# Hybrid encoder block: the branch gates' projections as seven half-size products per pair of feature tiles, in a stage of their own ahead of the mixers

## The chip, the cores and the metric

The kernel runs on one core of a Trainium2 chip. The metric is the device time of one execution in microseconds (us). The engines are named as in the profile: PE (TensorE matmuls) with PEld (its weight loads), DVE (VectorE), ACT (ScalarE), POOL (GpSimd), and SP, whose queue issues every DMA of this kernel.

## The reference

One layer of a bidirectional encoder: 1024 tokens, 1024 features, all in float32.

```
h = rms_norm(x)
q,k,v,r, lr_f,lr_b, sq,sk,sv, gate_a, gate_b = split(h @ w_in)
A = gla(q, k, v, lr_f, lr_b)            # 4 heads, both directions, chunks; rms_norm per head
A = (A * silu(r)) @ w_o_gla
B = windowed_attention(sq, sk, sv)      # 8 query heads, 2 kv heads, +-128 tokens, sinks
B = B @ w_o_swa
x = x + (sigmoid(gate_a) * A + sigmoid(gate_b) * B) @ w_out
x = x + (silu(h2 @ w1) * (h2 @ w2)) @ w_ffn_out        # h2 = rms_norm(x), 2816 wide
```

The change concerns `gate_a` and `gate_b`: 2048 of the columns of `h @ w_in`.

## The kernel before, in words

Activations lie with features on the partitions, in tiles of 128 features by 512 tokens, so that each of the 8 feature tiles has two halves s = 0, 1. Float32 products are made from fp32r parts: a tile is split into a rounded part (`wh`, `xh`: one ACT copy) and the rest (`wl`, `xl`: one DVE subtraction), and every block product is three matmuls, h·h, h·l and l·h (`mm3`, line 72). `wunit` (lines 62 to 69) loads 128 x 512 weights and splits them; the load goes into a ring of 4 buffers (`wr`), the halves into rings of 5 (`wh`, `wl`). PSUM is two pools of four banks, `mm` and `ch`.

The program runs through these stages.

1. Opening: the 16 tiles of x are loaded, scaled by the norm's gain and split. PE makes q0 and k0 behind them, then the gate codes (`lr_mm`) and the norm's statistics. 1/rms is a factor per token, `rstd`, multiplied in when a projection leaves PSUM.
2. Linear attention (GLA): 45 slots. Each slot runs some of `g_gates`, `g_scores`, `g_out`, `g_back_out` and `g_turn` for one chunk or another, a head's backward pass behind its forward one.
3. Windowed attention: 21 slots t. Step n (group g, block t) goes through `a_prep`, `a_turn`, `a_scores`, `a_probs` and `a_out` in slots n+1 to n+5; the keys are prepared in the first eight (`k_prep`, `k_turn`).
4. Merge: `prep_a(s)` loads the eight tiles of the GLA output (`lo`) and of r (`lr`), forms o·gain·r·sigmoid(r) and splits it into `oah` and `oal`; `branch_a(s)` multiplies by `w_o_gla` and by sigmoid(gate_a); `prep_b`, `branch_b` do the same for the attention; `out_proj` follows. `lo` and `lr` have two buffers each.
5. The feed-forward part. Its first layer (`ffn_in`) already computes each 2 x 2 block product (two feature tiles, two halves of tokens, two halves of the contraction) with seven half-size products on sums and differences of blocks, in place of eight.

The PE's order is the order in which the code is written (`manual_schedule`); the other engines and the SP queue get theirs from a scheduler that reads it. The attention steps leave PE little work, so `fill(n)` puts n matmuls out of a list of remaining projections (`dense`) between them. The list holds v, q1 to k3, the attention's keys, values and queries, r0 to r7 and last `ga0, gb0, ..., ga7, gb7`, 2400 matmuls in all, of which the gates are 768: 16 feature tiles of 48. What is left of the list after the last attention slot is run through by `fill(1 << 30)`, between the last `a_out` and `branch_a(0)`; in this kernel that is 191 matmuls.

Of the kernel before, what the change touches and what calls it, by code (L numbers as in the profile page):

```python
# [8 lines left out]
F32 = mybir.dt.float32  # L9
FR = mybir.dt.float32r  # L10
# [13 lines left out]
NB = 7  # L24
PAD = 672
# [4 lines left out]
def body(tc, i, out):  # L30
    nc = tc.nc
    with ExitStack() as root:
# [15 lines left out]
        def chtile(shape, dt=F32):  # L48
            return psc.tile(list(shape), dt, tag="ch", name=nm("ch"))

# [40 lines left out]
        def rsqrt(dst, v, scale, epsv, eps_t, pool, shape, tag):  # L91
            l = pool.tile(list(shape), F32, tag=tag + "l", name=nm("rl"))
            nc.scalar.activation(l, v, AF.Ln, bias=eps_t[:, 0:1], scale=scale)
            nc.scalar.activation(l, l, AF.Exp, scale=-0.5)
            t = pool.tile(list(shape), F32, tag=tag + "t", name=nm("rt"))
# [8 lines left out]
        stg = stgs.enter_context(tc.tile_pool(name="stg", bufs=4))  # L104
        pad = root.enter_context(tc.tile_pool(name="pad", bufs=1, side="right"))
        pad.tile([P, PAD // 4], F32, tag="pad", name="pad")
# [6 lines left out]
        gc = glas.enter_context(tc.tile_pool(name="gc", bufs=1))  # L113
        ini = ExitStack()
        ip = ini.enter_context(tc.tile_pool(name="ip", bufs=1))
        acc = ip.tile([P, T], F32, tag="acc", name="acc")
        def norm_stats(acc, pool):
            for s in range(2):
                v = chtile((P, HT))
                mm(v, ones, acc[:, s * HT:(s + 1) * HT], True, True)  # L120
                rsqrt(rstd[:, s * HT:(s + 1) * HT], v, 1.0 / T, EPS, epst, pool, (P, HT), "rs")

        def fgroup(units, xa, xb, nk):

            b = [mmtile(), mmtile()]
            k = 0
            for src, ku in units:
                h, l = wunit(src, ku * P)
                for kk in range(ku):
                    c = slice(kk * P, (kk + 1) * P)  # L130
                    st, sp = k == 0, k == nk - 1
                    mm(b[0], h[:, c], xa[k][0], st, False)
                    mm(b[0], h[:, c], xb[k][0], False, False)
                    mm(b[1], h[:, c], xa[k][1], st, False)
                    mm(b[1], h[:, c], xb[k][1], False, False)
                    mm(b[0], l[:, c], xa[k][0], False, sp)
                    mm(b[1], l[:, c], xa[k][1], False, sp)
                    k += 1
            return b

# [100 lines left out]
        lrS = gc.tile([98, T], FR, tag="lrS", name="lrS")  # L241
        upS = gc.tile([98, 2, 512], FR, tag="upS", name="upS")

        mask = gc.tile([P, 4, P], F32, tag="mask", name="mask")
        nc.vector.memset(mask, 1.0)
        nc.vector.memset(mask[:, :, 0:1], 0.0)
# [8 lines left out]
        def lr_out(b):  # L255
            lrf = ip.tile([96, T], F32, tag="lrf", name="lrf")
            for s in range(2):
                c = slice(s * HT, (s + 1) * HT)
                nc.vector.tensor_tensor(lrf[:, c], b[s][:96], rstd[:96, c], op=ALU.mult)
            nc.scalar.activation(lrS[0:96], lrf, AF.Copy)  # L260
            nc.vector.tensor_tensor(lrS[32:64], lrf[32:64], lrS[32:64].bitcast(F32), op=ALU.subtract)

        def x_tile(k, s):
            xr = ip.tile([P, HT], F32, tag="xr", name=nm("xr"), bufs=8)
            nc.sync.dma_start(out=xr, in_=i["xT"][k, s])
            nc.scalar.activation(xh[k][s], xr, AF.Copy, scale=g1[:, k:k + 1])  # L266
            nc.vector.scalar_tensor_tensor(xl[k][s], xr, g1[:, k:k + 1], xh[k][s].bitcast(F32),  # L267
                                           op0=ALU.mult, op1=ALU.subtract)
            a = acc[:, s * HT:(s + 1) * HT]
            sq = a if k == 0 else ip.tile([P, HT], F32, tag="sq", name=nm("sq"), bufs=3)  # L270
            nc.scalar.activation(sq, xr, AF.Square)
            if k:
                nc.vector.tensor_tensor(a, a, sq, op=ALU.add)

        with tc.manual_schedule(engines={mybir.EngineType.PE}):
            bq = [[mmtile(), mmtile()] for _ in range(2)]
            for k in range(KT):
                if k % 4 == 0:
                    us = [wunit(i["w_f"][m, k // 4]) for m in range(2)]
                c = slice((k % 4) * P, (k % 4 + 1) * P)  # L280
                for s in range(2):
                    x_tile(k, s)
# [3 lines left out]
            tri = load_const(gc, "tri", i["c_tri"], (P, P), U32)  # L286
# [3 lines left out]
            lr_mm(bl, 0)  # L290
            norm_stats(acc, ip)
            vt = chtile((P, KT, 2))
            for t in range(KT):
                mm(vt[:, t], acc[:, t * P:(t + 1) * P], ones[:, 0:2], True, True)
            lr_mm(bl, 1)
            proj_f_out("q0", bq[0])
            proj_f_out("k0", bq[1])
            rsqrt(rstdt, vt[:, :, 0], 1.0 / T, EPS, epst, ip, (P, KT), "rt")
            upr = ip.tile([98, 2, 512], F32, tag="upr", name="upr")
            nc.sync.dma_start(out=upr, in_=i["up"])  # L300
            nc.scalar.activation(upS, upr, AF.Copy)
            nc.vector.tensor_tensor(upS[64:98], upr[64:98], upS[64:98].bitcast(F32), op=ALU.subtract)
            nc.scalar.activation(upS[96:97], upr[96:97], AF.Copy)
            nc.vector.memset(lrS[96:98].bitcast(F32), 1.0)
            lr_out(bl)
# [11 lines left out]

        class Chunk:
            pass
# [3 lines left out]
        def g_gates(hd, c):  # L323
# [11 lines left out]
            nc.sync.dma_start(out=qk[:, 1], in_=scr[f"k{hd}", s][:, co:co + 256])  # L335
            z = chtile((P, 2, 256))
# [146 lines left out]
        for m in range(8):  # L483
            dense += [proj_f(f"ga{m}", 16 + m), proj_f(f"gb{m}", 24 + m)]
# [20 lines left out]
        swas = ExitStack()  # L505
        sc_ = swas.enter_context(tc.tile_pool(name="swc", bufs=1))
# [87 lines left out]
        def a_turn(g, n):  # L594
# [10 lines left out]
            a.p = sw.tile([P, 4, 384], F32, tag="p", name=nm("p"))  # L605
            a.mx = sw.tile([P, 4], F32, tag="mx", name=nm("mx"))

        def a_scores(g, n, h):
            a = att[g, n]
            w, p, mx = a.w, a.p, a.mx  # L610
# [158 lines left out]
        def gate(nme, s):  # L769
            g = btile(nme[:2])  # L770
            nc.sync.dma_start(out=g, in_=scr[nme, s])
            nc.scalar.activation(g, g, AF.Sigmoid)
# [63 lines left out]
        def wsplit(src, n):  # L836
            h = wp.tile([P, n], FR, tag="wh", name=nm("wh"), bufs=5)
            l = wp.tile([P, n], FR, tag="wl", name=nm("wl"), bufs=5)
            nc.scalar.activation(h, src, AF.Copy)  # L839
            nc.vector.tensor_tensor(l, src, h.bitcast(F32), op=ALU.subtract)  # L840
            return h, l

# [17 lines left out]

        def product(o, w, x, nk, start, stop):
            h, l = w
            for kk in range(nk):
                c = slice(kk * P, (kk + 1) * P)
                nc.tensor.matmul(o, h[:, c], x[kk][0], start=start and kk == 0, stop=False, skip_group_check=True)  # L865
                nc.tensor.matmul(o, h[:, c], x[kk][1], start=False, stop=False, skip_group_check=True)  # L866
                nc.tensor.matmul(o, l[:, c], x[kk][0], start=False, stop=kk == nk - 1, skip_group_check=True)  # L867
# [327 lines left out]
```

## Time and profile before

| | |
|---|---|
| median of 3 runs | 1697.69 us (1697.48 to 1699.71) |
| profiled execution: device time, and its span in the profile | 1697.71 us, 1695.6 us |
| busy share PE, PEld, DVE, ACT | 99%, 82%, 70%, 51% |
| matmuls | 7880 |
| opening, up to the GLA's first matmul | 0 to 53.9 us |
| the two attentions | 53.9 to 753.3 us |
| remaining projections | 753.3 to 796.6 us |
| merge and feed-forward | 796.6 to 1695.6 us |

The stages' borders are start times of PE instructions in the timeline. PE matmuls are pipelined: one of 512 columns shows some 0.39 us, but the next starts 0.227 us after it. So a busy share of PE says only that it rarely stood still for long; whether it waited is read from the distance of the starts.

### The profile page before, as it was taken

What the parts mean: (1) busy time and instruction counts of PE and PEld (TensorE: products, weight loads), DVE (VectorE), ACT (ScalarE), POOL (GpSimd) and SP (SyncE); (2) the same over time, 40 slices, a digit from 0 to 9 for tenths busy, and PEclk for the clock granted to TensorE, in tenths of its full rate; (3) what the DMA queues carried; (4) which work ended last, traced back from release to release, by engine and by line L of the source; (5) the groups of instructions that cost most, each with busy time, mean ns of one, the idle gap of its engine ahead of it and who ended that gap; (6) DMA issues with size and microseconds to landing.
All of it is one profiled execution on the core that took longest, in us unless ns stands there. A gap on an engine that the chain in (4) does not pass through costs nothing.

```text
span 1695.6 us, 23682 instructions
## 1 busy us (share of the span) xinstructions
PE 1675.2 (99%) x7880; PEld 1388.9 (82%) x7880; DVE 1179.8 (70%) x2454; ACT 867.8 (51%) x1939; POOL 0.2 (0%) x4
## 2 busy tenths in 40 slices
PE   8999999999999999999999999999999999999999
PEld 6788888888788878878888888888888888788887
DVE  7767777764577656537574468978778887779655
ACT  6554767775557565545453456633333333354443
POOL 0000000000000000000000000000000000000000
PEclk9999999999999999999999999999999999999999
DMA  6533444443543232237765645344223543496433
GB/s 196 156 112 111 121 130 135 132 143 119 177 128 108 82 106 81 82 108 249 237 200 168 192 137 180 116 128 149 88 94 131 172 157 129 138 342 200 142 106 118
DMA packets 153738, 245.85 MB, mean 145 GB/s; under 512 B 17582, under 2 KB 43054, under 8 KB 153616
## 3 DMA queue, kind: packets, MB, share of 16 engines
q1 hardware_dynamic: 153616, 244.34, 45.4%
q8 instruction: 62, 1.02, 0.3%
q14 instruction: 60, 0.49, 0.1%
HBM read 177.17 MB, written 67.11 MB: 144 GB/s over the span
## 4 chain that ended last, share of the span: by engine, by line
PE 92%; DVE 3%; ACT 3%; DMA 1%; issue 1%; SPq 0%; ACTq 0%; DVEq 0%
PE mm L72 46%; PE ch L72 8%; PE mm L1012 6%; PE mm L865 6%; PE mm L866 6%; PE mm L867 6%; PE ch L1012 5%; PE ch L866 2%; PE ch L867 2%; PE ch L865 2%; PE ch L647 1%; ACT p L636 1%; ACT p L630 1%; PE ch L474 0%; PE ch L389 0%
## 5 line engine op out<-in xcount | busy, mean ns | idle before, releaser
L66 ACT ACTIVATE wh<-wr 128x512 fp32r<-128x512 f32 (+1 forms) x256 | 159.2, 626 | 173.6 <-PE mm L72 149.2
L68 DVE TENSOR_TENSOR wl<-wr,wh 128x512 fp32r<-128x512 f32 (+1 forms) x256 | 174.6, 685 | 92.6 <-ACT wh L66 88.0
L72 PE MATMUL mm<-xh,wh 128*128 128x512 f32 x512 | 204.1, 399 | 6.5 <-ACT xh L266 6.5
L72 PE MATMUL mm<-xl,wh 128*128 128x512 f32 x512 | 204.0, 398 | 0.0
L72 PE MATMUL mm<-xh,wl 128*128 128x512 f32 x512 | 169.7, 398 | 0.0
L72 PE MATMUL mm<-wh,xh 128*128 128x512 f32 x320 | 126.7, 396 | 1.9 <-DVE st L146 1.2
L72 PE MATMUL mm<-wl,xh 128*128 128x512 f32 x320 | 127.3, 398 | 0.0
L72 PE MATMUL mm<-wh,xl 128*128 128x512 f32 x320 | 126.3, 395 | 0.0
L72 PEld LDWEIGHTS mm<-xh,wh 128*128 128x128 f32 x512 | 97.0, 190 | 23.3 <-ACT xh L266 6.5
L839 ACT ACTIVATE wh<-ws 128x512 fp32r<-128x512 f32 x88 | 55.5, 632 | 115.9 <-PE mm L866 68.0
L72 PEld LDWEIGHTS mm<-xl,wh 128*128 128x128 f32 x512 | 97.2, 190 | 17.5 <-DVE xl L267 0.5
L72 PEld LDWEIGHTS mm<-xh,wl 128*128 128x128 f32 x512 | 95.3, 190 | 16.7
L839 ACT ACTIVATE wh<-a 128x512 fp32r<-128x512 f32 x66 | 41.7, 632 | 89.8 <-PE ch L1012 42.3
L839 ACT ACTIVATE wh<-wr 128x512 fp32r<-128x512 f32 x52 | 32.9, 632 | 91.6 <-issue 49.7
L840 DVE TENSOR_TENSOR wl<-a,wh 128x512 fp32r<-128x512 f32 x66 | 45.5, 690 | 41.6 <-ACT wh L839 41.4
L72 PEld LDWEIGHTS mm<-wh,xh 128*128 128x128 f32 x320 | 60.2, 188 | 13.9 <-DVE st L146 1.6
L630 ACT ACTIVATE p<-p,nm,rs 128x384 f32<-128x384 f32 (+1 forms) x64 | 42.9, 672 | 56.1 <-DVE nm L624 56.1
L1012 PE MATMUL mm<-hh,wh 128*128 128x512 f32 x176 | 68.6, 390 | 1.5 <-ACT hh L984 1.5
L1012 PE MATMUL mm<-hl,wh 128*128 128x512 f32 x176 | 68.7, 390 | 0.8 <-DVE hl L985 0.8
L840 DVE TENSOR_TENSOR wl<-ws,wh 128x512 fp32r<-128x512 f32 x88 | 60.1, 683 | 12.5 <-ACT wh L839 12.5
L72 PEld LDWEIGHTS mm<-wh,xl 128*128 128x128 f32 x320 | 60.2, 188 | 10.4
L1012 PE MATMUL mm<-hh,wl 128*128 128x512 f32 x176 | 68.6, 390 | 0.1
(508 smaller groups left out, 4420.6 us busy)
## 6 DMA issues: line engine op xcount, KB each, us to landing
wr<-in_w_fi_dram SPq DMA_DIRECT2D x102, 256.0 KB, 2.8
wr<-in_w_t_dram SPq DMA_DIRECT2D x80, 256.0 KB, 2.7
wr<-in_w_f_dram SPq DMA_DIRECT2D x64, 256.0 KB, 2.7
B<-c SPq DMA_DIRECT2D x44, 256.0 KB, 2.1
T<-tx SPq DMA_DIRECT2D x44, 256.0 KB, 2.3
a<-in_w_fo_dram SPq DMA_DIRECT2D x44, 256.0 KB, 5.3
hr<-T SPq DMA_DIRECT2D x44, 256.0 KB, 2.7
hr<-B SPq DMA_DIRECT2D x33, 256.0 KB, 4.6
```

Of the source, the lines that this page charges most:

```text
L66: nc.scalar.activation(h, raw, AF.Copy)
L68: nc.vector.tensor_tensor(l, raw, h.bitcast(F32), op=ALU.subtract)
L72: nc.tensor.matmul(o, a, b, start=start, stop=stop)
L630: nc.scalar.activation(p[:, h, :w], p[:, h, :w], AF.Exp, bias=nm_[:, h:h + 1], scale=a.rs[:, h:h + 1], accum_out=dn[:, h:h + 1])
L636: nc.scalar.activation(p[:, h, :w], p[:, h, :w], AF.Copy, scale=rd[:, h:h + 1])
L647: nc.tensor.transpose(pt[:, h], a.p[:, h, (kb - a.b0) * P:(kb - a.b0 + 1) * P], ident)
L839: nc.scalar.activation(h, src, AF.Copy)
L840: nc.vector.tensor_tensor(l, src, h.bitcast(F32), op=ALU.subtract)
L865: nc.tensor.matmul(o, h[:, c], x[kk][0], start=start and kk == 0, stop=False, skip_group_check=True)
L866: nc.tensor.matmul(o, h[:, c], x[kk][1], start=False, stop=False, skip_group_check=True)
L867: nc.tensor.matmul(o, l[:, c], x[kk][0], start=False, stop=kk == nk - 1, skip_group_check=True)
L1012: nc.tensor.matmul(ys[m], a[:, c], b, start=f0, stop=f1, skip_group_check=True)
```

## The change

The sixteen gate tiles leave the list. Their products are made in a stage of their own behind the opening, for each pair (`ga` tile f, `gb` tile f) by seven products on blocks of x and w, as `ffn_in` does: `x_first(f)` makes the two that need no sums, `x_two`, `x_four` and `x_last` the five others. Sums of x are made once by `xcombos`, those of w for each pair by `w0comb`. The results go to DRAM without `rstd`, and `gate()` multiplies it in when it loads them. q0, k0 and the gate codes also go out raw (`keep_raw`), to be scaled when they are loaded. The opening loads x into 16 buffers of its own and begins with 12 small matmuls on ones; the constants and the gate-code tiles of the GLA (`lrS`, `upS`) are now allocated after the new stage, in the memory that it frees. The slots of both attentions get fewer matmuls of filling, and the windowed attention runs its steps within a slot in another order.

```diff
+        def x_first(f):
+            F = pairs[f]
+            Y = mmtile()
+            product(Y, wunit(i["w_f"][16 + f, 0]), X0["11"], 4, True, False)
+            F.p1 = ep.tile([P, HT], F32, tag=f"e{f}", name=nm("xp1")) if f < 4 else \
+                x0.tile([P, HT], F32, tag=f"xr{f - 4}1", name=nm("xp1"))
+            nc.scalar.copy(F.p1, Y)
+            product(Y, wunit(i["w_f"][16 + f, 1]), X0["21"], 4, False, True)
+            keep_raw(f"ga{f}", 0, Y)
...
+        def x_two(f):
+            F = pairs[f]
+            F.r11, F.r12, F.r21, F.r22 = (w0load(f, q) for q in (11, 12, 21, 22))
+            F.Z, F.X = chtile((P, HT)), mmtile()
+            s1 = w0comb(F.r21, F.r22, ALU.add)
+            product(F.Z, wsplit(s1, 512), X0["T1"], 4, True, False)
+            F.p5 = xtile("p5", f)
+            nc.scalar.copy(F.p5, F.Z)
+            nc.vector.tensor_tensor(F.p5, F.p5, F.p1, op=ALU.add)
+            F.s2 = w0comb(s1, F.r11, ALU.subtract)
+            product(F.X, wsplit(F.s2, 512), X0["T2"], 4, True, False)
+            F.u2 = xtile("u2", f)
+            nc.vector.tensor_tensor(F.u2, F.X, F.p1, op=ALU.add)
+
+        def x_four(f):
+            F = pairs[f]
+            s3 = w0comb(F.r11, F.r21, ALU.subtract)
+            product(F.X, wsplit(s3, 512), X0["T3"], 4, False, False)
...
+            product(F.Z, wsplit(s4, 512), X0["22"], 4, False, True)
+            nc.vector.tensor_tensor(F.u2, F.Z, F.u2, op=ALU.add)
+            keep(f"ga{f}", 1, F.u2)
+
+        def x_last(f):
+            F = pairs[f]
+            product(F.X, wsplit(F.r22, 512), X0["T4"], 4, False, True)
...
+            wu = chtile((P, 512))
+            for _ in range(12):
+                mm(wu[:, :P], ones, ones, True, True)
...
+            for f in range(NG):
+                x_first(f)
+                if f == 0:
...
+                for k in range(f, 4, 4):
+                    xcombos(k, 0)
+                for k in range(f - 4, 4, 4):
+                    if f >= 4:
+                        xcombos(k, 1)
+            for f in range(NG):
+                x_two(f)
...
+                if f:
+                    x_last(f - 1)
+                x_four(f)
+            x_last(NG - 1)
+        g0s.close()
+
+        gc = glas.enter_context(tc.tile_pool(name="gc", bufs=1))
+        lrS = gc.tile([98, T], FR, tag="lrS", name="lrS")
...
+        nc.sync.dma_start(out=upr, in_=i["up"])
+        nc.scalar.activation(upS, upr, AF.Copy)
+        nc.vector.tensor_tensor(upS[64:98], upr[64:98], upS[64:98].bitcast(F32), op=ALU.subtract)
+        nc.scalar.activation(upS[96:97], upr[96:97], AF.Copy)
...
+            nc.sync.dma_start(out=lrf[:, c], in_=scr["lr", s][:96])
+            nc.vector.tensor_tensor(lrf[:, c], lrf[:, c], rstd[:96, c], op=ALU.mult)
+        nc.scalar.activation(lrS[0:96], lrf, AF.Copy)
+        nc.vector.tensor_tensor(lrS[32:64], lrf[32:64], lrS[32:64].bitcast(F32), op=ALU.subtract)
...
-        for m in range(8):
+        for m in range(NG, 8):
             dense += [proj_f(f"ga{m}", 16 + m), proj_f(f"gb{m}", 24 + m)]
...
             fill(24)
             for t in range(last + 1):
-                n = 40 if t < 6 else 31 if t < NH * NC + 3 else 18
+                n = 40 if t < 6 else 26 if t < NH * NC + 3 else 12
...
-        order = (a_out, a_probs, a_scores, a_turn, k_turn, k_prep, a_prep)
+        order = (k_prep, a_prep, a_scores, a_turn, k_turn, a_out, a_probs)
...
-                slot([lambda e=e: e[0](*e[1:]) for e in v], 60 if t < 2 else 46 if t < 2 * KT + 2 else 28)
+                slot([lambda e=e: e[0](*e[1:]) for e in v], 36 if t < 2 else 24 if t < 2 * KT + 2 else 8)
...
+            if int(nme[2:]) < NG:
+                nc.vector.tensor_tensor(g, g, rstd[:, s * HT:(s + 1) * HT], op=ALU.mult)
             nc.scalar.activation(g, g, AF.Sigmoid)
```

Three places in the order of the engines. The first is ACT behind the gate codes. Before, it splits the first weights of the list there (`wh`), with the statistics between:

```order
L66 ACTIVATE wh_531<-wr_529 128x512
L66 ACTIVATE wh_537<-wr_535 128x512
L303 ACTIVATE upS<-upr 1x1024
L66 ACTIVATE wh_543<-wr_541 128x512
L66 ACTIVATE wh_561<-wr_559 128x512
L93 ACTIVATE rl_410<-ch_408,eps 128x512
```

Now the eight `x_first` stand there; three of them (`xp` is the copy of the first product out of PSUM, `c` that of the finished sum):

```order
L70 ACTIVATE wh_750<-wr_748 128x512
L320 COPY xp_101_638<-mm_619 128x512
L259 ACTIVATE T4h_935<-xr_302 128x512
L70 ACTIVATE wh_783<-wr_781 128x512
L309 COPY c_658<-mm_619 128x512
L70 ACTIVATE wh_803<-wr_801 128x512
L320 COPY xp_114_692<-mm_673 128x512
L70 ACTIVATE wh_836<-wr_834 128x512
L309 COPY c_712<-mm_673 128x512
L70 ACTIVATE wh_856<-wr_854 128x512
L320 COPY xp_127_746<-mm_727 128x512
```

Each copy `xp` stands behind a weight split; the ring of five gives that split (`wh_750`) the buffer that the same first product read last.

The second place is ACT in one slot of the windowed attention (`p`<-`p` with `dn`: exponentials of the four heads; `p`<-`p,rd`: division; `ph`: split of the turned probabilities; `sqh`: split of the turned queries; `sob`: the output). Before:

```order
L630 ACTIVATE p_8166,dn_8324<-p_8166,nm_8317,rs_8001 128x384
L627 ACTIVATE es_8321<-es_8321 128x4
L630 ACTIVATE p_8166,dn_8324<-p_8166,nm_8317,rs_8001 128x384 x3
L601 ACTIVATE sqh_8345<-ch_8340 128x512
L66 ACTIVATE wh_8597<-wr_8595 128x512
L636 ACTIVATE p_8166<-p_8166,rd_8330 128x384 x4
L661 COPY sob_8393<-ch_8383 128x512
L650 ACTIVATE ph_8424<-ch_8419 128x512
L650 ACTIVATE ph_8438<-ch_8433 128x512
L650 ACTIVATE ph_8451<-ch_8446 128x512
```

Now:

```order
L754 ACTIVATE sqh_8256<-ch_8251 128x512
L784 ACTIVATE p_8200,dn_8236<-p_8200,nm_8229,rs_7876 128x384
L781 ACTIVATE es_8233<-es_8233 128x4
L784 ACTIVATE p_8200,dn_8236<-p_8200,nm_8229,rs_7876 128x384 x3
L815 COPY sob_8272<-ch_8262 128x512
L790 ACTIVATE p_8200<-p_8200,rd_8242 128x384 x4
L804 ACTIVATE ph_8285<-ch_8280 128x512
L804 ACTIVATE ph_8303<-ch_8298 128x512
L804 ACTIVATE ph_8314<-ch_8309 128x512
L70 ACTIVATE wh_8593<-wr_8591 128x512
```

The three `ph` behind the division were those of the block just divided; now they are those of the block before it, which PE turned without waiting for this division.

The third place is the SP queue behind the last attention output, where the loads of `prep_a` have begun (`lo`, `lr`, `lo` stand ahead of these rows in both). Before:

```order
L755 DMA lr_9448<-r_0_5842 128x512
L771 DMA ga_9530<-ga_0_7055 128x512
L64 DMA wr_9552<-in_w_oa_dram 128x512
L771 DMA ga_9571<-ga_0_7461 128x512
L771 DMA gb_10002<-gb_0_7271 128x512
L771 DMA gb_10048<-gb_0_7646 128x512
L150 DMA ga_0_9186<-st_9187 128x512
L150 DMA ga_1_9190<-st_9191 128x512
L755 DMA lr_9460<-r_0_5943 128x512
```

Now:

```order
L909 DMA lr_9746<-r_0_8136 128x512
L925 DMA ga_9828<-ga_0_515 128x512
L925 DMA ga_9870<-ga_0_606 128x512
L68 DMA wr_9977<-in_w_oa_dram 128x512
L925 DMA gb_10308<-gb_0_1102 128x512
L925 DMA gb_10355<-gb_0_1216 128x512
L956 DMA lx_11068<-in_xT_dram 128x512
L126 DMA r_0_9682<-st_9683 128x512
L126 DMA r_1_9686<-st_9687 128x512
L909 DMA lr_9758<-r_0_8436 128x512
```

The last projection to be stored was a gate (`ga_0`, `ga_1`), with others behind it; now it is r7 (`r_0`, `r_1`), the last of the list, which the same `prep_a` needs. On PE, 50 matmuls stand between the last `a_out` and `branch_a(0)`, where 191 stood.

More of the change, by code (lines that the diff above doesn't have):

```diff
@@ L24 @@
 NB = 7
+NG = 8
 PAD = 672
@@ L263, in x_tile @@
[L263 to L271, printed above, removed]
-            if k:
-                nc.vector.tensor_tensor(a, a, sq, op=ALU.add)
+        g0s = ExitStack()
@@ new lines, in x_split, with x_square @@
+        def x_split(h, l, r, g):
+            nc.scalar.activation(h, r, AF.Copy, scale=g)
+            nc.vector.scalar_tensor_tensor(l, r, g, h.bitcast(F32), op0=ALU.mult, op1=ALU.subtract)
+        acc = [ep.tile([P, HT], F32, tag=f"e{2 + s}", name=f"acc{s}") for s in range(2)]
+        def x_square(k, s):
+            sq = acc[s] if k == 0 else ep.tile([P, HT], F32, tag=f"e{k % 2}", name=nm("sq"))
+            nc.scalar.activation(sq, xr[k, s], AF.Square)
+            if k:
+                nc.vector.tensor_tensor(acc[s], acc[s], sq, op=ALU.add)
@@ new lines, in product, with keep @@
+        def product(o, w, x, nk, start, stop):
+            h, l = w
+            for kk in range(nk):
+                c = slice(kk * P, (kk + 1) * P)
+                nc.tensor.matmul(o, h[:, c], x[kk][0], start=start and kk == 0, stop=False, skip_group_check=True)
+                nc.tensor.matmul(o, h[:, c], x[kk][1], start=False, stop=False, skip_group_check=True)
+                nc.tensor.matmul(o, l[:, c], x[kk][0], start=False, stop=kk == nk - 1, skip_group_check=True)
+        def keep(name, s, t):
+            d = scratch(f"{name}_{s}")
+            nc.sync.dma_start(out=d[:t.shape[0]], in_=t)
+            scr[name, s] = d
@@ new lines, in keep_raw @@
+        def keep_raw(name, s, b, n=P):
+            c = ep.tile([P, HT], F32, tag="c", name=nm("c"), bufs=2)
+            nc.scalar.copy(c[:n], b[:n])
+            keep(name, s, c[:n])
+        pairs = [Chunk() for _ in range(NG)]
+        def x_first(f):
[7 more added lines that the diff above has]
+            keep_raw(f"ga{f}", 0, Y)
@@ L275, in body @@
+        def x_last(f):
+            F = pairs[f]
+            product(F.X, wsplit(F.r22, 512), X0["T4"], 4, False, True)
+            c21 = xtile("c21", f)
+            nc.vector.tensor_tensor(c21, F.X, F.p1, op=ALU.add)
+            keep(f"gb{f}", 0, c21)
         with tc.manual_schedule(engines={mybir.EngineType.PE}):
+            xr[0, 0] = x_load(0, 0)
+            wu = chtile((P, 512))
+            for _ in range(12):
+                mm(wu[:, :P], ones, ones, True, True)
             bq = [[mmtile(), mmtile()] for _ in range(2)]
+            us = [wunit(i["w_f"][m, 0]) for m in range(2)]
+            xr[0, 1] = x_load(0, 1)
@@ L289, in body @@
             bl = [chtile((P, 512)), chtile((P, 512))]
[L290 to L305, printed above, removed]
+            for u in range(2):
+                lr_mm(bl, u)
+            for m in range(2):
+                for s in range(2):
+                    keep_raw(("q0", "k0")[m], s, bq[m][s])
@@ new lines, in body @@
+        ini = ExitStack()
+        ip = ini.enter_context(tc.tile_pool(name="ip", bufs=1))
+        upr = ip.tile([98, 2, 512], F32, tag="upr", name="upr")
+        nc.sync.dma_start(out=upr, in_=i["up"])
+        nc.scalar.activation(upS, upr, AF.Copy)
+        nc.vector.tensor_tensor(upS[64:98], upr[64:98], upS[64:98].bitcast(F32), op=ALU.subtract)
+        nc.scalar.activation(upS[96:97], upr[96:97], AF.Copy)
+        nc.vector.memset(lrS[96:98].bitcast(F32), 1.0)
+        lrf = ip.tile([96, T], F32, tag="lrf", name="lrf")
@@ L859, in comb @@
             return t
[L861 to L867, printed above, removed]
         home = {"a": ("01", "11", "21", "31", "41", "51", "61", "71"),
```

162 lines of the change are left out of this document (106 added, 56 removed).

## The prediction

> **What bounds the kernel.** I read the page first, then the busy time in single stretches, then PE's waits, the chain that ended last, and the timeline at the places that the change touches.
>
> ```profile
> span 1695.6 us, 23682 instructions
> PE 1675.2 (99%) x7880; PEld 1388.9 (82%) x7880; DVE 1179.8 (70%) x2454; ACT 867.8 (51%) x1939; POOL 0.2 (0%) x4
> ```
>
> The sum below is made against this execution, 1697.7 us with 2.1 around its span; the median of the runs is the same 1697.7. In the stretches the columns are PE, PEld, DVE, ACT and POOL, with the number of instructions:
>
> ```profile
> 190.00:351.40 161.40, 161.40 (x902) 138.42 (x901) 122.86 (x336) 119.11 (x324) 0.00 (x0) 1.00 0.44 134
> 441.00:485.00 44.00, 44.00 (x201) 36.10 (x200) 33.20 (x117) 21.91 (x98) 0.00 (x0) 1.00 0.57 175
> 535.00:720.40 185.40, 183.79 (x911) 152.46 (x910) 112.91 (x328) 108.33 (x310) 0.00 (x0) 1.00 0.28 88
> 990.00:1486.00 496.00, 493.81 (x2174) 407.45 (x2173) 395.61 (x638) 200.24 (x333) 0.00 (x0) 1.00 0.41 135
> ```
>
> The first is 16 GLA slots, the second the first three attention slots, the third 11 later ones, the fourth the feed-forward with its seven products. PE is full in each. Of PE's waits between 60 and 753 us the largest are these (line waited for, total, times, longest):
>
> ```profile
> PE ch L647 <- ACT p L636: 1.9, 11, 0.2
> PE ch L474 <- ACT ob L468: 1.6, 1, 1.6
> ```
>
> So the mixers wait for nothing but PE, because filling covers them. The chain gives PE's pace:
>
> ```profile
> 6.46 25.15 PE mm L72 x96
> ...
> 31.61 6.41 PE ch L72 x26
> ...
> 753.44 233.73 PE mm L72 x1031
> ```
>
> 233.73/1031 = 0.2267 us a matmul of 512 columns. Fewer matmuls are time saved, as long as nothing else makes PE wait.
>
> **What goes.** Eight pairs of 96 matmuls become eight of 84: 96 x 0.2267 = -21.8 us. The opening: its 96 matmuls take 25.15 us where 21.8 would do. This is why:
>
> ```profile
> 6.46 0.79 PE L72 MATMUL mm<-xh,wh 128*128 128x512 f32 x1 [6.46 <-ACT xh L266]
> ...
> 8.26 0.63 PE L72 MATMUL mm<-xh,wh 128*128 128x512 f32 x1
> 8.69 0.63 PE L72 MATMUL mm<-xl,wh 128*128 128x512 f32 x1
> ...
> 12.82 0.40 PE L72 MATMUL mm<-xh,wl 128*128 128x512 f32 x1
> 13.05 0.40 PE L72 MATMUL mm<-xh,wh 128*128 128x512 f32 x1
> ...
> 47.38 0.39 PE L72 MATMUL mm<-wh,xl 128*128 128x512 f32 x1
> 48.97 0.50 PE L72 MATMUL mm<-wh,xh 128*128 128x512 f32 x1 [1.20 <-DVE st L146]
> 49.31 0.40 PE L72 MATMUL mm<-wl,xh 128*128 128x512 f32 x1
> ```
>
> After 6.46 us of standing still PE starts a matmul every 0.43 us (8.26 to 8.69) and reaches its pace some 6.1 us after its first; that costs 3.3 us, though the granted clock reads 1.00 in every stretch. After standing 1.2 us at 48.97 it is at pace at once. The twelve matmuls on ones, from about 1 us on, use up the slow time. I take most of it, with 0.7 us for an earlier first tile and 0.9 for a later second: -3.1 (from 0 to -3.5). Behind it, up to the GLA's first matmul at 53.9, 22.3 us hold 72 matmuls (16.3) and 2.3 of statistics; the other 3.7 are waits of an arrangement that goes: -3.7. Together -28.6.
>
> **x_first.** In each, the second product adds onto the bank that ACT must first have copied (`xp`), and nothing stands between the two on PE. In ACT's order a weight split, waiting for the same product, stands ahead of the copy.
>
> ```profile
> L66 ACT ACTIVATE wh<-wr 128x512 fp32r<-128x512 f32 x254 | 158.2, 627 | 173.6 <-PE mm L72 149.2 <-issue 8.1 <-PE ch L72 6.1
> L930 ACT COPY p<-ch 128x512 f32<-128x512 f32 x22 | 12.5, 567 | 0.0
> 764.25 0.62 ACT L772 ACTIVATE ga<-ga 128x512 f32<-128x512 f32 x1
> 764.77 0.61 ACT L757 ACTIVATE sg<-lr 128x512 f32<-128x512 f32 x1
> ```
>
> From the start of the product's last matmul: 0.39 to its end, 0.53 for the split (ACT starts one every 0.52), 0.57 for the copy, some 0.1 of signals: 1.58, less the 0.23 that PE would need anyway = 1.35 us, eight times. At f = 0 ACT also has sums of x ahead of it: 0.6 more. The first T3 waits for a DVE read with nothing in between: 1.0. Sum +12.4; without the split +7. The DVE and ACT work of the five other products (14 x 0.69 and 6 x 0.6 us per 13.6 of PE) is 71% and 26%; the same scheme in the feed-forward runs without PE waits at 80% of DVE, so it costs nothing. Its DMAs (7 x 256 KB per 13.6 us, 135 GB/s) are no more than that stage's 135.
>
> **Into the GLA.** `upr` and `lrf` now load into memory that the last stores of the new stage free. Behind PE's last product: c21 0.9 us, its store 2.2, `lrf` 0.5 to issue behind `upr` and 2.3 to land = 6.9; the splits of `upS` (1.06 and 1.22 us by the rows of the equally long `lrS`, twice ACT) and `lrS` follow one another on ACT and DVE up to about 12.2.
>
> ```profile
> 50.74 1.06 ACT L260 ACTIVATE lrS<-lrf 96x1024 fp32r<-96x1024 f32 x1 [3.22 <-DVE lrf L259]
> 51.84 1.22 DVE L261 TENSOR_TENSOR lrS<-lrf,lrS 32x1024 fp32r<-32x1024 f32 x1 [1.13 <-ACT lrS L260]
> ga<-st SPq DMA_DIRECT2D x16, 256.0 KB, 2.2
> qk<-k SPq DMA_DIRECT2D x16, 128.0 KB, 2.3
> ```
>
> PE has 24 matmuls (5.4) until the gates' matmul needs `lrS`: +6.7 (3 to 9).
>
> **The slots.** GLA: 16 slots lose 80 matmuls, 18.1 of 161.4 us; DVE keeps 122.9 less 7 splits, so it rises from 76% to 83%. Each step feeds one a slot or more later: +2 over the stage (0 to 9). Attention: 22 matmuls fewer in each of 16 slots. In the first three, 96 instead of 166 leave PE some 28 us; DVE had 33.2, less 4 for six splits. DVE leads from there while keys are prepared: +1.2 a slot for six slots, 7. Later slots hold 5.9 us of PE's own and 24 x 0.227 = 11.4. Against that stands a loop, since PSUM's four `ch` banks turn over: the fourth scores, DVE to `nm` (0.61 and 1.8 of other work in its order), exponentials 2.8, the output's copy 0.6, division 2.1, three `ph` 1.7, `pl` 0.7, the next fourth scores 0.7 to 1.7: 11.3 to 12.3.
>
> ```profile
> 677.20 2.08 ACT p L630 x6
> ...
> 680.19 2.13 ACT p L636 x4
> L650 ACT ACTIVATE ph<-ch 128x512 fp32r<-128x512 f32 x31 | 18.4, 592 | 6.1 <-PE ch L647 5.7
> L651 DVE TENSOR_TENSOR pl<-ch,ph 128x512 fp32r<-128x512 f32 x32 | 22.1, 689 | 26.7 <-ACT ph L650 26.5
> L615 DVE CUSTOM_DVE_ANT_0 p<-ch,band 128x384 f32<-128x384 f32 (+1 forms) x44 | 23.4, 532 | 28.5 <-PE ch L72 28.2
> ```
>
> (Six records of L630 are three exponentials.) About +0.5 in ten slots, 5. Attention together +12, from 2 where ACT and DVE run ahead to 24 where the loop and the key slots each take 1 us more.
>
> **The hand-over.** Timeline around the last `a_out`:
>
> ```profile
> 753.04 0.39 PE L72 MATMUL ch<-ph,vSl 128*128 128x512 f32 x1
> ...
> 754.09 1.79 SPq L663 DMA_DIRECT2D b<-sob  x4
> 757.47 0.32 SPq L753 DMA_DIRECT2D lo<-o  x1
> 766.52 0.63 ACT L745 ACTIVATE oah<-lo 128x512 fp32r<-128x512 f32 x1
> 786.97 0.63 ACT L745 ACTIVATE oah<-lo 128x512 fp32r<-128x512 f32 x1 [0.76 <-DVE lo L759]
> 788.65 0.68 DVE L746 TENSOR_TENSOR oal<-lo,oah 128x512 fp32r<-128x512 f32 x1
> ...
> 796.61 0.39 PE L72 MATMUL mm<-oah,wh 128*128 128x512 f32 x1
> ```
>
> With T0 = 753.3, `lo` loads when the last `sob` is stored (T0+4.2), the first piece is split at T0+13.2, the eighth done at T0+36.1, two pieces per 6.5 us through the two buffers of `lo` and `lr`. The 191 matmuls reach T0+43.3: hidden by 7 us. Now 50 reach T0+11.3, and the first group of 24, which needs all eight pieces, could end at T0+16.7. The loads wait for the same stores; the third `lr` stands in SP's queue behind r7's store, which comes at T0+12.8, no later than it was issued before (766.5). So pieces come as before, the group ends 0.45 after the eighth, near T0+36, and PE loses 19; I take 18.5 (13 if the pieces come at 1.4 us less a pair, 20 if r7 is late). `gate()`'s 32 multiplications, 0.69 each, lie beside PE's work of the merge, and DVE's mean share of the span is 70%: nothing.
>
> A PE that stands for that long starts slowly: nearest row the opening, 3.3 us; nearest below the 1.2 at 48.97, none. I take +3.3 once, here, where it stands in pieces of 3 us; the 6.7 ahead of the GLA is open (0 to 3.3).
>
> The Trainium skill, TensorE: Matmul & The Clock Gate, section What's actually happening, says that an idle window of about 3.4 us puts the array's clock back to half, and sustained work of that length restores it. The opening's rows agree (0.43 against 0.227). By the rule both long waits would be followed by half pace, and the sum be 1727; by the rows alone it is the one below. No run here shows the clock behind such a wait.
>
> **Sum.** -28.6 + 12.4 + 6.7 + 2 + 12 + 18.5 + 3.3 = +26.3: 1697.7 + 26.3 = 1724.0 us.
>
> **Rivals.** (1) The mixers stay PE-bound: PE hardly waits there now, and the new order gives the softmax a whole slot more. Against it: DVE at 83% and the loop. It takes away 2 + 12: 1710. (2) The hand-over is covered and the kernel faster: pieces of `prep_a` come ahead of the last slots. It takes away 18.5 + 3.3, 1702.2; it decides the sign once the slots add under 9.5 (28.6 - 12.4 - 6.7), and gives 1690 with their lower end, 2. For it: ACT is half idle there. Against: in the rows the first load waits for the last store. (3) ACT and DVE set the attention's pace: 24 instead of 12 and a slow restart ahead of the GLA as well, 1739. That the change doesn't do what it says is no rival: the order has 84 matmuls fewer, which is 96 less the twelve on ones.
>
> **Chances.** Forecast 0.58, (1) 0.16, (2) 0.13, (3) 0.13. The range takes all but the lower half of (2) and what lies beyond (3): 1701 to 1741. Within 0.2% (3.4 us, about what a measurement tells from no change) is 1694.3 to 1701.1. Of (2), half is faster, a quarter the same: faster 0.08; same 0.05 with 0.02 from a cheaper (1); slower 0.87.
>
> **What would show it.** In the profile after: distances of 1.6 us on PE in the middle of every `x_first`; the GLA's first matmul near 218 us and PE idle ahead of it, waiting for `lrS`; attention slots near 12 us with PE waiting for `p` or for banks; PE between the last `a_out` and the second `w_o_gla` group idle for 18 us on `oah`; matmuls 0.43 us apart behind it. The feed-forward should take the same time as now. I am wrong if pieces of `oah` come sooner than two per 6.5 us, or if the slots run at PE's pace.

## The result, and the profile after

The changed kernel takes 1725.18 us (median of 4 runs, 1723.14 to 1726.76) where the kernel before, run beside it, took 1697.88: ratio 1.0158, 95% interval 1.014 to 1.0176. It is slower by 27 us; 1724.0 was forecast. The first lines of its page:

```profile
span 1721.4 us, 23818 instructions
PE 1671.7 (97%) x7808; PEld 1375.7 (80%) x7808; DVE 1253.2 (73%) x2591; ACT 909.9 (53%) x2017; POOL 0.2 (0%) x4
```

PE still seems full. What it waits for (line waited for, total us, times, longest) says otherwise:

```profile
PE mm L76 <- ACT oah L899: 10.1, 7, 3.4
PE mm L298 <- ACT xp L320: 8.0, 8, 1.2
PE ch L76 <- DVE lrS L455: 7.6, 1, 7.6
PE ch L626 <- ACT ob L620: 2.3, 1, 2.3
PE ch L76 <- ACT ph L804: 2.1, 2, 1.3
```

Before, the longest wait in the mixers was 1.6 us. Three new ones lead, at the three places where the change set new borders. The stretches around the wait for `lrS` and around the hand-over (PE, PEld, DVE, ACT, POOL, then the granted clock, the DMA share, GB/s):

```profile
207.30:220.60 13.30, 5.65 (x26) 4.37 (x24) 6.49 (x8) 5.04 (x6) 0.00 (x0) 0.83 0.52 158
220.60:230.00 9.40, 9.40 (x31) 7.60 (x32) 7.48 (x20) 5.30 (x10) 0.00 (x0) 0.70 0.27 85
...
786.60:801.60 15.00, 11.68 (x52) 9.30 (x50) 6.50 (x11) 5.56 (x8) 0.00 (x0) 1.00 0.79 271
801.60:824.00 22.40, 14.42 (x23) 5.77 (x24) 17.78 (x28) 11.23 (x19) 0.00 (x0) 0.53 0.82 252
824.00:845.00 21.00, 21.00 (x87) 17.24 (x88) 14.41 (x23) 10.62 (x18) 0.00 (x0) 0.93 0.70 221
```

220.6 to 230 shows how a busy share deceives: 9.40 of 9.40 us busy, but only 31 matmuls, at a clock of 0.70. So I count otherwise below. The *excess* of a stretch is its length less what its matmuls take at pace (0.227 us for 512 columns, 0.175 for 384, 0.119 for 256, 0.110 for 128, the smallest usual distances of starts in these traces). It holds waits and slow clock alike. The GLA is taken to end with its last matmul (the turning of `ob`), and the attention to run from there to its last `a_out`. By stage, after minus before, both from the profiled executions, with the prediction's terms:

| term | predicted | measured |
|---|---|---|
| 96 matmuls of 512 columns fewer | -21.8 | -21.8 |
| opening: slow clock | -3.1 | -0.8 (e5) |
| opening: old waits | -3.7 | -3.7 |
| x_first (10.1, e3) and the first T3 (0.8) | +12.4 | +10.9 |
| wait ahead of the GLA | +6.7 | +7.8 |
| slow clock behind it | 0, open to 3.3 | +2.6 |
| GLA | +2 | +3.0 |
| attention | +12 | +3.5 |
| hand-over: wait, and slow clock behind it | +18.5, +3.3 | +20.1, +2.1 |
| rest of the merge, feed-forward | 0 | +2.0 |
| sum | +26.3 | +25.7 (spans: 1695.6 to 1721.4) |

The row "old waits" was not measured by itself: it is what the opening and the new stage together leave (+6.4, the time of the ones counted as waiting) when the rows of the clock and of x_first are taken off.

The timeline in one `x_first`, PE and ACT together: the last matmuls of the first product, the split that stands ahead of the copy, the copy, and the first matmul of the second product:

```profile
59.66 0.39 PE L300 MATMUL mm<-xh,wl 128*128 128x512 f32 x1
59.86 0.63 ACT L70 ACTIVATE wh<-wr 128x512 fp32r<-128x512 f32 x1 [1.08 <-PE mm L299]
60.40 0.57 ACT L320 COPY xp<-mm 128x512 f32<-128x512 f32 x1
61.02 0.50 PE L298 MATMUL mm<-xh,wh 128*128 128x512 f32 x1 [0.97 <-ACT xp L320]
```

From start to start 1.36 us, 1.13 more than PE needs. The timeline at the hand-over, after the last `a_out` at T0 = 786.7:

```profile
797.67 0.61 PE L76 MATMUL mm<-xh,wl 128*128 128x512 f32 x2
801.64 0.50 PE L76 MATMUL mm<-oah,wh 128*128 128x512 f32 x1 [3.36 <-ACT oah L899]
...
822.26 0.61 ACT L899 ACTIVATE oah<-lo 128x512 fp32r<-128x512 f32 x1
...
822.93 0.79 PE L76 MATMUL mm<-oah,wh 128*128 128x512 f32 x1 [1.28 <-ACT oah L899]
```

The filling ends at T0+11.4; the eighth piece of `oah` is split at T0+35.6, and PE follows the pieces one by one.

### The profile page after: what moved, and what is told of

It is laid out like the page before. It is cut to its first block, busy times and chain, and to the rows that moved or that the text cites. A ratio compares the mean times of both kernels' runs of the same rounds, so it can differ in the third digit from the quotient of the medians.

```text
span 1721.4 us, 23818 instructions
## 1 busy us (share of the span) xinstructions
PE 1671.7 (97%) x7808; PEld 1375.7 (80%) x7808; DVE 1253.2 (73%) x2591; ACT 909.9 (53%) x2017; POOL 0.2 (0%) x4
## 4 chain that ended last, share of the span: by engine, by line
PE 73%; DVE 5%; ACT 4%; DMA 3%; issue 1%; SPq 0%; DVEq 0%; ACTq 0%
PE mm L76 30%; PE ch L76 7%; PE mm L1153 6%; PE mm L298 5%; PE mm L299 5%; PE mm L300 5%; PE ch L1153 5%; PE ch L299 2%; PE ch L298 2%; PE ch L300 2%; PE ch L801 1%; DMA lo<-o 1%; DMA ga<-ga 1%; DMA kvr<-skv 0%; DMA lr<-r 0%
## 5 line engine op out<-in xcount | busy, mean ns | idle before, releaser
L72 DVE TENSOR_TENSOR wl<-wr,wh 128x512 fp32r<-128x512 f32 (+1 forms) x240 | 164.0, 686 | 74.6 <-ACT wh L70 73.5
L290 ACT ACTIVATE wh<-ws 128x512 fp32r<-128x512 f32 x120 | 76.0, 634 | 182.3 <-PE mm L299 85.6
L291 DVE TENSOR_TENSOR wl<-ws,wh 128x512 fp32r<-128x512 f32 x120 | 82.3, 686 | 29.2 <-ACT wh L290 29.1
L76 PE MATMUL mm<-xh,wh 128*128 128x512 f32 x256 | 102.8, 401 | 0.4 <-ACT wh L70 0.4
L76 PE MATMUL mm<-xl,wh 128*128 128x512 f32 x256 | 102.7, 401 | 0.1
L76 PE MATMUL mm<-xh,wl 128*128 128x512 f32 x256 | 85.3, 399 | 0.0
L76 PEld LDWEIGHTS mm<-wh,xh 128*128 128x128 f32 x320 | 60.9, 190 | 10.9 <-ACT st L186 1.0
L76 PEld LDWEIGHTS mm<-wl,xh 128*128 128x128 f32 x320 | 60.8, 190 | 10.0
L76 PE MATMUL mm<-oah,wh 128*128 128x512 f32 x128 | 53.2, 416 | 10.3 <-ACT oah L899 10.1
L1126 DVE TENSOR_TENSOR hl<-hr,hh 128x512 fp32r<-128x512 f32 x77 | 52.7, 685 | 5.3 <-ACT hh L1125 5.3
L76 PEld LDWEIGHTS mm<-xh,wh 128*128 128x128 f32 x256 | 48.2, 188 | 7.7 <-ACT wh L70 0.5
```

The source lines that it names most:

```text
L72: nc.vector.tensor_tensor(l, raw, h.bitcast(F32), op=ALU.subtract)
L76: nc.tensor.matmul(o, a, b, start=start, stop=stop)
L1126: nc.vector.tensor_tensor(l, r, h.bitcast(F32), op=ALU.subtract)
```

## The experiments

Each starts from the changed kernel; times are medians, spans those of the profiled executions. The theory throughout is that of the sum above: three separate waits with their clock, and little else. The rival is that a wait taken away comes back elsewhere, since the mixers have lost their cover.

**e1: seven pairs in the new stage.**

```diff
-NG = 8
+NG = 7
+            for k in range(max(NG - 4, 0), 4):
+                xcombos(k, 1)
```

> Seven pairs in the new stage; the eighth pair's 96 matmuls stand behind r7 at the end of the list of filling, so 146 matmuls instead of 50 run between the last a_out and the first w_o_gla group. Theory (PE stands still at the hand-over only because too little filling is left, and the eight pieces of oah come at the pace of their loads): the excess there falls from 22 us to about 4, against 12 matmuls more of work (+2.7) and one x_first less (-1.0): about -16 us against the changed kernel, 1709. Rival (the pieces of oah share ACT, DVE and the DMA queue with the filling's splits and stores, and come later with it): the wait moves behind the filling, the gain is 8 us or less, 1717 or more.

Measured: 1708.54 us, 16.6 less. The stretches from the last `a_out` to the first `w_o_gla` matmul, and through branch_a(0), and ACT's last piece:

```profile
770.30:803.70 33.40, 33.40 (x149) 27.63 (x148) 23.08 (x37) 15.63 (x26) 0.00 (x0) 1.00 0.78 258
803.70:847.20 43.50, 43.50 (x194) 36.03 (x193) 32.18 (x51) 21.17 (x39) 0.00 (x0) 1.00 0.83 266
```

```profile
805.63 0.63 ACT L901 ACTIVATE oah<-lo 128x512 fp32r<-128x512 f32 x1 [1.20 <-DVE lo L915]
```

The eighth piece comes at T0+35.1 (T0 = 770.5), as without the filling, and PE now gets there just then: the excess of the hand-over falls from 22.2 to nothing. The pieces come no later with 96 matmuls more beside them; the rival falls.

**e2: PE kept busy in the wait for lrS.**

```diff
             fill(24)
+            wu = chtile((P, 512))
+            for _ in range(34):
+                mm(wu[:, :P], ones, ones, True, True)
             for t in range(last + 1):
```

> The changed kernel with 34 small matmuls on ones behind the 24 that stand ahead of the GLA, that is, about 7 us of PE work that nothing needs, in the 7.65 us in which PE waits for lrS. Theory (the half pace behind that wait is the clock, lowered because PE stood still): the wait shrinks to about 0.5, the granted clock behind it reads 1.00 where it read 0.70, and the 3.1 us of slow matmuls go: 1722. Rival (the first matmuls of the GLA are slow because of their operands): the matmuls behind the wait still start every 0.43 us, no gain, 1725.

Measured: 1722.76 us (1719.7 to 1725.24). The two stretches that answer to those of the changed kernel:

```profile
207.50:220.60 13.10, 13.10 (x93) 12.05 (x91) 6.49 (x8) 5.02 (x6) 0.00 (x0) 1.00 0.53 162
220.60:230.00 9.40, 9.40 (x43) 7.83 (x43) 7.70 (x21) 5.92 (x11) 0.00 (x0) 1.00 0.37 113
```

The GLA's first matmul still comes at 220.6, since `lrS` does; but the 9.4 us behind it hold 43 instead of 31 matmuls, at a clock of 1.00. Work that nobody needs, in 7 us of waiting, saves 2.6 us of excess. The slow stretch is a matter of the clock, not of operands. (In whole runs 2.4 us is not clear of the spread; the trace of this place is.)

**e3: the two products of x_first apart.**

```diff
+            x_one(0)
             for f in range(NG):
+                if f + 1 < NG:
+                    x_one(f + 1)
                 x_first(f)
```

(`x_one` is the first half of the old `x_first`, up to the copy; `x_first` keeps the second product.)

> In the new stage the first product of pair f+1 stands on PE between the two products of pair f, so that the copy of the bank has 2.7 us of cover; nothing else is changed. Theory (the bubbles are the wait for the copy, 8.0 us in the changed kernel): PE's waits for xp go to 0.5 us or less, 1717.5. Rival (the bubble is set by ACT's order, a split and a copy for every product whatever the distance, or by weights coming late): the distances stay or turn into waits for wh, less than 3 us gained, 1722 or more.

Measured: 1716.04 us, 9.1 less; the excess from 0 to the GLA's boundary falls by 10.1. No wait for `xp` is left among PE's waits, which are now led by

```profile
PE mm L76 <- ACT oah L905: 10.9, 6, 4.1
PE ch L76 <- DVE lrS L461: 7.7, 1, 7.7
```

So a step of 12 matmuls of other work covers the copy, split ahead of it and all.

**e4: filling ahead of the GLA.**

```diff
-            fill(24)
+            fill(60)
-                n = 40 if t < 6 else 26 if t < NH * NC + 3 else 12
+                n = 40 if t < 6 else 25 if t < NH * NC + 3 else 11
```

> 60 instead of 24 matmuls of filling ahead of the GLA's first step, paid for by one matmul less in 39 of the 45 GLA slots (26 to 25, 12 to 11); what is left at the end changes by three. Theory (the GLA slots are still bound by PE, so a matmul moved out of them costs them nothing; the wait for lrS is all cover): PE's wait of 7.65 and the 3.1 of slow clock behind it go, nothing comes back: 1714.5. Rival (the GLA's own chains set the slots' pace by now, and each slot keeps its length when it loses a matmul): 39 x 0.227 = 8.8 us come back as waits in the GLA, only the clock's 3.1 remain as a gain: 1722.

Measured: 1707.15 us, 18.0 less, more than either expected. The stretches before and behind the GLA's first matmul:

```profile
206.50:220.30 13.80, 13.80 (x63) 11.22 (x61) 7.12 (x10) 6.12 (x8) 0.00 (x0) 1.00 0.60 172
220.30:230.00 9.70, 9.70 (x46) 8.10 (x46) 7.69 (x19) 6.33 (x12) 0.00 (x0) 1.00 0.60 189
```

The wait and the slow clock are gone. The gain beyond that: `need`, which runs filling until a projection is stored, had to run less, so the GLA lost 62 matmuls instead of 39 (1942 against 2004 records between its first matmul and the first scores), and 26 came to stand at the hand-over, whose excess fell from 22.2 to 16.7. Nothing came back in the GLA: its excess without the slow clock went from 14.6 to 12.7 (up to the first scores). The GLA is bound by PE.

**e5: no matmuls on ones.** The edit takes the twelve and their tile out of the opening.

> The changed kernel without the twelve matmuls on ones at its start. Theory (they use up the slow time of a PE that has stood still, so q0's and k0's first matmuls run at pace): the first product matmuls start every 0.43 us again for some 6 us and the opening is 3 us longer: 1728. Rival (the opening is set by the arrival and the splitting of x, 16 tiles one after the other, and PE's pace in its first microseconds doesn't matter): no change, 1725.

Measured: 1726.43 us, ratio to before 1.0168 (1.0153 to 1.0183), not told apart from the changed kernel by whole runs. PE's first matmuls:

```profile
6.21 0.80 PE L76 MATMUL mm<-xh,wh 128*128 128x512 f32 x1 [6.21 <-ACT wh L70]
...
8.94 0.62 PE L76 MATMUL mm<-xh,wh 128*128 128x512 f32 x1
9.36 0.44 PE L76 MATMUL mm<-xl,wh 128*128 128x512 f32 x1
9.64 0.39 PE L76 MATMUL mm<-xh,wl 128*128 128x512 f32 x1
```

They are slow, but for 3.2 us and seven matmuls, not for 6.1 us and fourteen as in the kernel before. Up to the end of the new stage the excess, the time of the ones counted as waiting, is 0.8 us larger. My theory (3 us) fails here and the rival is nearly right: the opening gives 0.8 to the clock.

**e6: the old order of the attention's steps.**

```diff
-        order = (k_prep, a_prep, a_scores, a_turn, k_turn, a_out, a_probs)
+        order = (a_out, a_probs, a_scores, a_turn, k_turn, k_prep, a_prep)
```

> The changed kernel with the attention's steps in the old order within a slot (a_out, a_probs, a_scores, a_turn, k_turn, k_prep, a_prep), filling as in the changed kernel. Theory (with 24 instead of 46 matmuls of filling the old order leaves 4 us of PE work between the fourth scores and the next a_probs, and the softmax chain between them takes 7.5): PE waits some 3.5 us for p in each of about 13 slots, +45 us, 1770. Rival (PE's waits in the attention come from elsewhere, and the order matters little): +10 us or less, 1735 or less.

Measured: 1784.13 us, 59 more than the changed kernel and 14 more than the theory had; the rival falls. PE's first wait:

```profile
PE ch L801 <- ACT p L790: 34.9, 52, 3.5
```

The excess in the attention is 71 instead of 16 us. The new order is what lets the slots do with 24 matmuls; it is the part of the change that holds the attention's loss at 3.5.

**e7: thinner attention slots.**

```diff
-[...], 36 if t < 2 else 24 if t < 2 * KT + 2 else 8)
+[...], 36 if t < 2 else 16 if t < 2 * KT + 2 else 0)
```

> The changed kernel with 16 instead of 24 matmuls of filling in the attention's slots and none instead of 8 in its last ones: 134 matmuls leave the attention, 194 instead of 50 stand ahead of the first w_o_gla group. The hand-over's 22 us go in any case. Theory of the prediction (ACT and DVE hold a slot at 11.3 us or more, which 24 matmuls just fill): the slots keep their length, the attention's excess over PE's pace rises by some 25 us, sum about 1728. Rival (the slots are still bound by PE at 24, and the loop is shorter than estimated): the excess rises by 5 us or less, 1708.

Measured: 1727.31 us, 2 more than the changed kernel: between the two. The attention's excess rises by 16.1, the hand-over's falls by 11.6 only (why, e8 shows). Four slots with key preparation and seven later ones, of the changed kernel:

```profile
624.69:670.98 46.29, 46.29 (x249) 39.38 (x249) 44.31 (x167) 46.12 (x159) 0.00 (x0) 1.00 0.35 109
682.51:761.61 79.10, 78.48 (x415) 65.79 (x413) 55.53 (x180) 61.19 (x173) 0.00 (x0) 1.00 0.27 87
```

and the same slots with 16 matmuls:

```profile
617.14:663.99 46.85, 41.44 (x219) 33.14 (x219) 44.00 (x170) 46.62 (x151) 0.00 (x0) 1.00 0.37 120
673.79:742.77 68.98, 66.64 (x358) 55.12 (x357) 51.67 (x178) 60.94 (x181) 0.00 (x0) 1.00 0.26 77
```

The four key slots keep their length: ACT is busy for 46.12 of 46.29 and 46.62 of 46.85 us and sets it, at 11.6 a slot; PE with 24 matmuls needs just as long. The later slots shrink from 11.3 to 9.85 us: there the loop that I put at 11.3 to 12.3 is no longer than 9.9.

**e8: all three waits at once.** The edits of e3 and e4, with 23 and 9 in the GLA's slots in place of 25 and 11.

> The changed kernel with the first product of pair f+1 between the two of pair f, 60 matmuls of filling ahead of the GLA, and 23 and 9 instead of 26 and 12 in its slots: 138 matmuls leave the GLA against the changed kernel, 36 stand in the wait for lrS, 152 instead of 50 ahead of the first w_o_gla group. Theory (the three waits add up and nothing else was lost; the GLA is bound by PE down to 23): -9.5, -10.3 and -22: 1683, below the kernel before by 0.8%. Rival (the GLA's slots are set by DVE below 25): 76 matmuls, 17 us, come back as waits in the GLA: 1700.

Measured: 1696.91 us (ratio to before 0.9997, 0.9987 to 1.0007). Neither was right. The GLA stayed bound by PE (excess 15.0 up to the first scores; 14.6 in the changed kernel without the slow clock), so its rival falls; but the hand-over kept 10.9 us of excess with 152 matmuls of cover. The timelines of SP, ACT and PE there:

```profile
783.68 0.86 SPq L126 DMA_DIRECT2D r<-st  x2
...
787.24 0.38 SPq L915 DMA_DIRECT2D lr<-r  x1
...
792.84 0.61 ACT L905 ACTIVATE oah<-lo 128x512 fp32r<-128x512 f32 x1
```

```profile
785.58 0.39 PE L76 MATMUL mm<-oah,wl 128*128 128x512 f32 x1
793.51 0.79 PE L76 MATMUL mm<-oah,wh 128*128 128x512 f32 x1 [7.54 <-ACT oah L905]
```

The last projection of the list is r7, which the eighth piece needs. Its way, store, load, three operations, begins when the filling ends, however much filling there is: 7.5 us of waiting, and 3.4 of slow clock behind it (the list of e1 ended with a gate, so there r7 had long been stored). Besides, the attention's excess is 4.4 us larger than in the changed kernel, which stays unexplained.

**e9: seven pairs, and all three waits.** NG = 7 with the edits of e3 and e4.

> e8_all_waits had 152 matmuls ahead of the first w_o_gla group, and PE waited 7.5 us there for the eighth oah, because r7, last of the list, was stored only when the filling was over. Here seven pairs are made in the new stage (25 and 11 in the GLA's slots, 60 ahead of it, the first products apart): the eighth pair's projections stand behind r7, which is stored some 22 us before the filling ends; 172 matmuls ahead of the first w_o_gla group. Theory (r7's way through the queue is the whole of that wait): no excess at the hand-over, 10.9 us less than e8, against 2.7 us more of work and one first product less: 1688. Rival (the eight pieces come late for another reason, the two buffers or the DMA queue): a wait of 5 us or more stays at the hand-over, 1695.

Measured: 1687.48 us, ratio to before 0.993 (0.9918 to 0.9942), the fastest of all here with e11. The theory holds: the hand-over has no excess, as the stretches from the last `a_out` to the first `w_o_gla` matmul and through branch_a(0) show:

```profile
741.80:781.10 39.30, 39.30 (x175) 32.50 (x174) 27.36 (x43) 19.12 (x32) 0.00 (x0) 1.00 0.77 248
781.10:824.60 43.50, 43.50 (x194) 36.02 (x193) 28.85 (x46) 18.89 (x34) 0.00 (x0) 1.00 0.79 244
```

What leads PE's waits is a new one, in branch_b:

```profile
PE mm L76 <- DVE wl L72: 3.6, 1, 3.6
```

**e10: r4 to r7 half by half, eight pairs.**

```diff
+        dense += [proj_h(f"r{m}", 8 + m, s) for s in range(2) for m in range(4, 8)]
```

(in place of r4 to r7 in the list, on e8; `proj_h` makes one half of the tokens)

> e8_all_waits with all eight pairs in the new stage, but r4 to r7 made half by half: the first 512 tokens of the four, then the second 512, so that all that the first merge step needs is stored 96 matmuls before the filling ends. The price is eight weight units loaded and split once more. Theory (r7 late): the wait of 7.5 and the 3.4 of slow clock behind it go, 1686. Rival (the eight weight units more, or the pieces' own pace, take it back): 1694 or more.

Measured: 1692.6 us, ratio to before 0.9968 (0.9956 to 0.9979), between the theory's 1686 and the rival's 1694. The cause named in e8 holds: the hand-over's excess falls from 10.9 to 0.7. But 3.6 us came back between the GLA's end and the first scores, and 4.0 in the merge, where PE waits 2.6 us for `wl` as in e9; that the eight weight units do it was not tried alone.

**e11: the gates' rstd on POOL.** e9 with `nc.gpsimd` for the multiplication in `gate()`.

> e9_seven_all with the gates' multiplication by rstd (28 of them, in the merge) on POOL, which is idle, in place of DVE; everything else as in e9_seven_all, where PE waits 3.6 us for a weight half wl behind a queue of DVE work at 843.8 us and runs at half pace for 5 us behind it, 6.75 us of excess in the merge's second part. Theory (the 0.69 us multiplications, costed at nothing in the prediction, fill DVE just there): that excess falls to 1 us, 1682. Rival (the queue on DVE is prep_a(1) and branch_b alone, or POOL is slower and the gates come late): 1686 to 1690.

Measured: 1686.88 us, ratio 0.9936 (0.9924 to 0.9948): the same as e9. The wait stays:

```profile
PE mm L76 <- DVE wl L72: 4.7, 2, 4.3
```

So the multiplications are not what fills DVE there. The timeline of e9 says the same: DVE is busy without a break from 835.4 us until the missing `wl` begins at 847.1, with `prep_a(1)` and `branch_b`, and one multiplication (0.68 us) stands among these operations. But e11 isn't free of a cost of its own. The timelines of POOL and DVE in e11, ahead of the `wl` that PE waits for:

```profile
846.20 1.35 POOL L935 TENSOR_TENSOR gb<-gb,rstd 128x512 f32<-128x512 f32 x1 [11.17 <-DMA gb<-gb]
```

```profile
846.35 1.75 DVE L953 TENSOR_TENSOR gb<-gb,xg 128x512 f32<-128x512 f32 x1
848.02 0.68 DVE L72 TENSOR_TENSOR wl<-wr,wh 128x512 fp32r<-128x512 f32 x1
```

The DVE operation that begins beside the multiplication on POOL takes 1.75 us instead of 0.68 and holds `wl` back by 1.1. Without that the wait would still be some 3 us (an estimate: 4.3 less 1.1), so the theory falls all the same. The wait, and the slow clock behind it, remain open: some 6 us that a better order of the merge might gain.

## Why the prediction was right

The sum came within 1.2 us of the median. Of the large terms, the work, the hand-over, x_first and the wait ahead of the GLA came within 1.5 us each; the attention did not.

- **Work** came out as counted.
- **x_first** measured 10.1 instead of 11.4: the distance is 1.36 (1.63 at f = 0) where I had 1.58, since the split waits for the last matmul that reads `wh`, which is the one before the last, and starts 0.20 us after the last one's start, not 0.4. A little comes back, as the second matmul behind each of these waits starts after 0.34 us, not 0.23. Mechanism and cure are shown by e3.
- **Into the GLA**: 7.8 for 6.7, at 220.6 where 218 was forecast. The terms listed for the way of `lrf` add up to 5.9 us, not to 6.9, and `lrf` took 4.2 and 4.7 us to land where 2.3 was put: two errors that partly cancel. The clock behind it, left open at 0 to 3.3, was 2.6. By the rule of the Trainium skill, TensorE: Matmul & The Clock Gate, section What's actually happening, a wait of this length has to be followed by half pace; e2 agrees (0.70 without work in the wait, 1.00 with it), and the sum should have held it here. The length isn't that of this section of the Trainium skill, which gives about 3.4 us of sustained work for the way back: here the half pace lasted 5.7.
- **The hand-over**: the eighth piece done at T0+36.9 for T0+36.1, the excess 22.2 for 21.8. That cover alone was lacking is shown by e1; that r7's store can take its place as the last wait, which the prediction gave 1.5 us, by e8 and e10.
- **The attention** is the step that failed: "About +0.5 in ten slots" and "+1.2 a slot for six slots", 12 in all, measured 3.5. The prediction's own sign of being wrong, slots at PE's pace, came true here: the excess of the stretches shown under e7 is 0.3 us a key slot and 0.4 a later one. In the later slots the loop of banks is at most 9.9 us, not 11.3 to 12.3 (e7); its listed terms add up to 11.0 to 12.0. In the key slots I named DVE; ACT is the full engine, and at 24 matmuls PE and ACT balance. Rival (1) was right for the mixers' pace, without changing the result.
- **The opening's clock** gave 0.8 instead of 3.1 (e5): I took the fourteen slow matmuls of one trace for what the ones would save.

The closeness of the total is in part luck. The attention was put 8.5 too high and x_first 1.5; against that stand 2.3 too little for the opening's clock, 2.6 for the clock behind `lrS`, 1.1 for the wait ahead of it, 1.0 for the GLA and 2.0 for the late stages that I had at nothing.

## What to carry to other kernels

Work that is cut out of a PE-bound kernel was often the cover of something: before the saving is counted, find each wait that the filling hid (here a copy out of PSUM, a reload into freed memory, a chain of loads at a stage's end) and move filling there first; the same seven products for seven of the eight pairs, with that done, run 0.7% faster than the kernel before instead of 1.6% slower. Of a list of filling, the last item should be one that nobody waits for. And a slot can be thinned only down to its fullest other engine, which the windows of exactly those slots name.

## What the runs showed of the hardware

The slow stretch behind a wait varies in length: matmuls started every 0.43 us for 5.7 us behind the 7.65 us wait for `lrS` (220.6 to 226.3), for 6.1 us behind e8's 7.5 (793.5 to 799.6), for 5.3 us behind e9's 3.6 (847.8 to 853.1), for 3.2 us in e5's opening and 6.1 in that of the kernel before. Each costs about half its length (2.6 of 5.7, 3.4 of 6.1). The granted clock shows it inside the program (0.70), but read 1.00 over e5's first 13 us, in which the first starts are 0.43 us apart. Small matmuls on ones are enough to hold the clock (e2).

A multiplication of 128x512 on POOL takes 1.3 us where DVE takes 0.69, and it isn't free for DVE: in e11 an operation of DVE on two SBUF tiles that begins during one of them ends 0.5 to 0.7 us after it and takes up to 1.79 us in place of 0.68, while those that read PSUM keep 0.68 to 0.69.
